# Channel mixer of a streaming-encoder block: gate/up pairs as Strassen products, and GpSimd's weight sums at another place

## The chip, the cores and the metric

The kernel runs on one core of a Trainium2 chip. TensorE (PE) multiplies, with weight loads (PEld) that overlap it; VectorE (DVE), ScalarE (ACT) and GpSimd (POOL) work element by element; DMAs are issued from the queues of SyncE (SP), ACT and POOL. The metric is the device time of one execution in microseconds, the median of several runs.

## The reference

One layer of a residual block on x (512 tokens by 1024 channels, float32). Cut to what matters here:

```python
h = rmsnorm(x, norm1_w)
proj = h @ w_in                                # q, k, v, z, b, a, glu, gates
out_a = gated delta rule, gated norm, @ dn_w_o
c = silu(layernorm(causal_conv31(ga * sigmoid(gb)) + b))
out_b = c @ cm_w_pw2 + cm_b_pw2
x = x + (gate_a * out_a + gate_b * out_b) @ w_out
h2 = rmsnorm(x, norm2_w)
f_gate, f_up = split(h2 @ ffn_w_gate_up)       # 1024 -> 2 x 2816
x = x + (silu(f_gate) * f_up) @ ffn_w_down     # 2816 -> 1024
return rmsnorm(x, norm_f_w)
```

## The kernel before

All products are float32 in three parts. An operand x is split into a high part hi (ACT, a copy rounded to fp32r) and a low part lo = x - hi (DVE, two SBUF inputs), and `split3` (line 107) issues three matmuls: hi by hi, hi by lo, lo by hi. Weights come in units of 128x1024 (`unit`, line 92): a load on SP's queue into `raw`, `whi` on ACT, `wlo` on DVE, each with three buffers. `col_tile` (line 115) multiplies one unit (8 k-steps of 128) with 512 tokens: 24 matmuls of 512 columns.

The program goes through stages. First the input projection with the delta-rule heads and the 31-tap convolution. Then `ln_mean` (line 559) ends the convolution's statistics: GpSimd adds seven squares into `vacc`. The eight columns of `wo` follow, with `ln_norm` (line 575: one reciprocal, then eight products `cv <- cv,pa` on DVE and eight Silu on ACT) in between; the split of its result into `yh` and `yl` reuses the buffers of `wo`'s operand as PE is done with them. Then the eight columns of `wpw`, and `w_out` by tokens (`tok_mm`), whose result is added to x in `y1` and kept in SBUF. `norm2` and `transposes` bring h2 into channel-major form as `hh` and `hl`, in the buffers that the input projection used.

The channel mixer (line 868) runs over f = 0 to 21. Each pair is two columns of 1024, gate `pg` and up `pu`, 48 matmuls of 512 columns; then Silu on ACT and the product `fm` on DVE. For f below 11 = FK, `sums(f)` loads a 1 MB tile `wst` of the down projection's weights on POOL's queue, makes four sums of 128x512 in place on GpSimd and stores them in `wsum`.

The down projection is a product of 2x2 blocks by Strassen's seven products (in Winograd's form) already: halves of the 22 hidden tiles by halves of the tokens, and halves of the hidden tiles by halves of the output. It runs as three passes over FK = 11 units of two products each (`two`, line 931) and a last product, `p3`. Each pass prepares the next operand set (`set2`, `set3`, `set4`) behind its own products. `norm_f` (line 906) makes the closing norm of a token tile and its two output DMAs.

The order of instructions on an engine follows the code and a scheduler's priorities; each engine and each DMA queue takes its instructions in order, and a wait holds up all that is behind it. A tile of a pool with n buffers can't be written until the readers of the tile n before it are done.

Of the kernel before, what the change touches and what calls it, by code (L numbers as in the profile page):

```python
# [6 lines left out]
F32 = mybir.dt.float32  # L7
# [7 lines left out]
P = 128  # L15
T = 512
# [7 lines left out]
PAD3 = 368  # L24
START = 84
# [5 lines left out]
def block_kernel(ctx, tc, a):  # L31
# [6 lines left out]
    pa_ = ctx.enter_context(tc.tile_pool(name="pA", bufs=1))  # L38
# [52 lines left out]

    def unit(ap):
        n = 1024
        raw = wp.tile([P, 1024], F32, name="raw")
        if isinstance(ap, tuple):
            n = T * len(ap)
            for i, p in enumerate(ap):
                nc.sync.dma_start(raw[:, i * T:(i + 1) * T], p)
        else:
            nc.sync.dma_start(raw.rearrange("p (a c) -> p a c", a=2) if len(ap.shape) == 3 else raw, ap)  # L100
        hi = wp.tile([P, 1024], F32R, name="whi")
        marked(S.activation(hi[:, 0:n], raw[:, 0:n], AF.Copy), "unit")  # L102
        lo = wp.tile([P, 1024], F32R, name="wlo")
        marked(V.tensor_tensor(out=lo[:, 0:n], in0=raw[:, 0:n], in1=hi[:, 0:n].bitcast(F32), op=ALU.subtract), "unit")  # L104
        return hi, lo
# [22 lines left out]
    ph1 = ctx.enter_context(ExitStack())  # L128
    psg = ph1.enter_context(tc.tile_pool(name="psg", bufs=2, space=PSUM))
# [7 lines left out]
    with tc.tile_pool(name="st", bufs=2) as st:  # L137
# [74 lines left out]
        def glu0(i):  # L212
# [3 lines left out]
            c = tp.tile([P, T + 30], F32, name="c", bufs=3)  # L216
# [341 lines left out]

    def ln_mean():
# [5 lines left out]
        for i in range(KD):  # L565
# [3 lines left out]
            else:  # L569
                sq2 = tp.tile([P, T], F32, name="acc4")  # L570
                S.activation(sq2, cv[i], AF.Square)
                G.tensor_tensor(out=vacc, in0=vacc, in1=sq2, op=ALU.add)
# [142 lines left out]
    mp.tile([P, PAD], F32, name="pad", bufs=1)  # L715
# [15 lines left out]
    for j in range(KD):  # L731
# [3 lines left out]
        col_tile(ps, a["wo"][j], oh, ol)  # L735
        ma = mp.tile([P, T], F32, name="ma", bufs=KD + 1)
# [19 lines left out]


# [29 lines left out]
    def rms_half(ss, hf, n, cs, sq, last):  # L787
# [44 lines left out]

    tok_mm("wout", KD, mh, ml, norm2, transposes)
    ph2.close()
    keep.close()


    fp = ctx.enter_context(tc.tile_pool(name="fp", bufs=2))
    nfw = fp.tile([P, D], F32, name="nfw", bufs=1)
    nc.gpsimd.dma_start(nfw, a["nfw"].partition_broadcast(P))  # L840
    FK = FF // 2

    def xset():

        return fp.tile([P, T], F32R, name="fh", bufs=FK + 2), fp.tile([P, T], F32R, name="fl", bufs=FK + 2)

# [3 lines left out]

    wsum = [dram.tile([P, 4, T], F32, name="wsum", bufs=FK) for _ in range(FK)]

    def sums(k):
        r = fp.tile([P, 4, T], F32, name="wst", bufs=1)
        nc.gpsimd.dma_start(r, a["wdn"][k].rearrange("p (i c) -> p i c", i=4))
        b11, b12, b21, b22 = (r[:, i, :] for i in range(4))
        G.tensor_tensor(out=b11, in0=b12, in1=b11, op=ALU.subtract)
        G.tensor_tensor(out=b12, in0=b22, in1=b12, op=ALU.subtract)  # L860
        G.tensor_tensor(out=b22, in0=b22, in1=b11, op=ALU.subtract)
        G.tensor_tensor(out=b21, in0=b22, in1=b21, op=ALU.subtract)
        nc.gpsimd.dma_start(wsum[k], r)

    TH = T // 2
    t1, t2 = slice(0, TH), slice(TH, T)
    fms, set1 = [], []
    for f in range(FF):
# [6 lines left out]
        sg = fp.tile([P, T], F32, name="fsg")  # L875
# [5 lines left out]
        fm = fp.tile([P, T], F32, name="fm", bufs=FF)  # L881
        fms.append(fm)
        V.tensor_tensor(out=fm, in0=pu, in1=sg, op=ALU.mult)  # L883
        if f < FK:
            sums(f)
            set1.append(xset())
            hi, lo = (t[:, t1] for t in set1[f])
            xsplit(hi, lo, fm[:, t1])
        else:

            b = fms[f - FK]
            s1 = fp.tile([P, TH], F32, name="s1")
            V.tensor_tensor(out=s1, in0=b[:, t2], in1=fm[:, t2], op=ALU.add)
            hi, lo = (t[:, t2] for t in set1[f - FK])
            xsplit(hi, lo, s1)
            V.tensor_tensor(out=b[:, t2], in0=b[:, t1], in1=b[:, t2], op=ALU.subtract)
            V.tensor_tensor(out=b[:, t1], in0=s1, in1=b[:, t1], op=ALU.subtract)


    hps.close()  # L900
    dp = ctx.enter_context(tc.tile_pool(name="dp", bufs=2, side="right"))
    ss3 = dp.tile([P, 5, NT], F32, name="ss3", bufs=1)
    o0 = [dp.tile([P, T], F32, name="o0", bufs=NT) for _ in range(NT)]
    c1, c2 = slice(0, T), slice(T, D)

    def norm_f(hf, n, cs):
        last = hf == 4 or hf == 1 and n != 1
        rms_half(ss3, hf, n, cs, dp.tile([P, T], F32, name="rms_sq", bufs=1)[:, 0:cs.stop - cs.start], last)
        rs = ss3[:, 3, n:n + 1]
        if hf == 0:  # L910
            G.tensor_tensor(out=o0[n], in0=y1[:, n, cs], in1=nfw[:, cs], op=ALU.mult)
        if last:
            S.activation(o0[n], o0[n], AF.Copy, scale=rs)
            o1 = dp.tile([P, T], F32, name="o1")
            V.scalar_tensor_tensor(out=o1, in0=y1[:, n, c2], scalar=rs, in1=nfw[:, c2], op0=ALU.mult, op1=ALU.mult)
            nc.scalar.dma_start(a["out"][n][:, c1], o0[n])
            nc.sync.dma_start(a["out"][n][:, c2], o1)

    def add(n, cs, what, op=ALU.add, eng=V):
        eng.tensor_tensor(out=y1[:, n, cs], in0=y1[:, n, cs], in1=what, op=op)  # L920
# [149 lines left out]
```

## Time and profile before

| | |
|---|---|
| median of 3 runs | 1000.03 us (997.23 to 1003.04) |
| profiled execution | 1000.16 us, its span 998.4 us |
| mean granted TensorE clock | 0.987 |
| instructions | 13414 |
| HBM read, written | 119.52 MB, 18.10 MB |
| layer norm's statistics, `wo`, `wpw` | about 500 to 590 us |
| `w_out` and norm | about 590 to 643 us |
| channel mixer | about 643 to 870 us |
| down projection | about 870 to 990 us |

How to read it: the span runs from the first to the last instruction; the rest of the execution's time lies around it. Busy time is the time in which an engine worked on instructions of the program. PE's instructions are pipelined: the duration of one (0.39 us for 512 columns) is longer than the step from one start to the next, and the step is what counts in a row of them. A timeline row has the start, the duration, the engine, the line, the operation, the tiles (out<-in) and shapes, and in brackets how long the engine was idle before and who released it. L104 is the split of a weight unit on DVE, L102 the one on ACT, L113 a matmul.

### The profile page before, as it was taken

To read this page: it belongs to the slowest core of one execution; us is meant where nothing else is said; L and a number is where in the kernel's file an instruction comes from. 1 tells how busy PE (TensorE), PEld (TensorE's weight loads), DVE (VectorE), ACT (ScalarE), POOL (GpSimd) and SP (SyncE) were. 2 spreads that over 40 slices of the span, in tenths; PEclk is the share of its full clock that TensorE was granted. 3 is DMA by queue.
4 is the path that set the end of the run, shared out by engine and by line. 5 is a ranking of instruction groups with operands and counts; after the bars stand their busy time and mean duration, and the time that the engine had idled before them with its cause. 6 is when DMAs were issued, how large, how long until landed. Compare 5 with 4: busy or idle time off the path is not lost.

```text
span 998.4 us, 13414 instructions
## 1 busy us (share of the span) xinstructions
PE 963.2 (96%) x4775; PEld 790.2 (79%) x4775; DVE 680.7 (68%) x1044; ACT 508.4 (51%) x1053; POOL 302.1 (30%) x410
## 2 busy tenths in 40 slices
PE   7999889999999999999999999999999999999995
PEld 5687778787887888888878888888888888888784
DVE  4879688899769769998487644643344546468963
ACT  6597366867777665533456322422222322356543
POOL 0423836273453633000040000143534332001412
PEclk9999989999999999999999999999999999999997
DMA  8233323223041222233644432356565664256562
GB/s 320 90 107 97 97 64 97 59 81 117 27 134 58 93 87 64 96 117 134 239 165 148 141 124 85 119 201 241 210 238 195 233 228 143 90 168 191 158 210 84
DMA packets 48290, 138.49 MB, mean 139 GB/s; under 512 B 7472, under 2 KB 9424, under 8 KB 45408
## 3 DMA queue, kind: packets, MB, share of 16 engines
q1 hardware_dynamic: 44016, 112.36, 34.4%
q0 software_dynamic: 3488, 24.17, 6.7%
q10 hardware_dynamic: 720, 1.11, 0.3%
q8 instruction: 37, 0.61, 0.3%
q14 instruction: 29, 0.24, 0.1%
HBM read 119.52 MB, written 18.10 MB: 138 GB/s over the span
## 4 chain that ended last, share of the span: by engine, by line
PE 80%; DVE 9%; POOL 4%; ACT 3%; issue 3%; DMA 1%; SPq 0%; POOLq 0%; ACTq 0%; DVEq 0%
PE mm L113 60%; PE w L113 11%; DVE cv L543 3%; DVE wlo L104 2%; DVE acc L299 1%; POOL Un L349 1%; POOL ytm L375 1%; PE g L345 1%; PE st L482 1%; PE st L494 1%; PE b L414 1%; PE b L420 1%; PE st L480 1%; PE sp L487 1%; ACT Un L348 1%
## 5 line engine op out<-in xcount | busy, mean ns | idle before, releaser
L102 ACT ACTIVATE whi<-raw 128x1024 fp32r<-128x1024 f32 x167 | 176.2, 1057 | 318.5 <-PE mm L113 185.9
L113 PE MATMUL mm<-hh,whi 128*128 128x512 f32 x816 | 328.6, 403 | 0.0
L113 PE MATMUL mm<-hl,whi 128*128 128x512 f32 x816 | 323.4, 396 | 2.3 <-POOL hl L228 1.6
L113 PE MATMUL mm<-hh,wlo 128*128 128x512 f32 x816 | 323.2, 396 | 0.7 <-DVE wlo L104 0.7
L104 DVE TENSOR_TENSOR wlo<-raw,whi 128x1024 fp32r<-128x1024 f32 x167 | 214.4, 1285 | 120.8 <-ACT whi L102 120.2
L543 DVE SCALAR_TENSOR_TENSOR cv<-c,c31w,cv 128x512 f32<-128x512 f32 x240 | 186.5, 803 | 2.1
L113 PEld LDWEIGHTS mm<-hl,whi 128*128 128x128 f32 x816 | 154.5, 189 | 33.0 <-POOL hl L228 2.9
L113 PEld LDWEIGHTS mm<-hh,wlo 128*128 128x128 f32 x816 | 154.2, 189 | 32.7 <-DVE wlo L104 1.1
L113 PEld LDWEIGHTS mm<-hh,whi 128*128 128x128 f32 x816 | 154.5, 189 | 28.7 <-ACT hh L227 0.2
L375 POOL TENSOR_TENSOR ytm<-U,y 128x60 f32<-128x60 f32 (+14 forms) x120 | 57.3, 477 | 44.9 <-DMA U<-sc 36.2
L883 DVE TENSOR_TENSOR fm<-mm,fsg 128x512 f32<-128x512 f32 x21 | 14.5, 692 | 64.9 <-PE mm L113 64.9
L377 POOL TENSOR_TENSOR y<-y,ytm 128x60 f32<-128x60 f32 (+14 forms) x120 | 53.1, 442 | 9.3
L299 DVE SCALAR_TENSOR_TENSOR acc<-mm,c4w,acc 128x511 f32<-128x511 f32 (+2 forms) x72 | 53.2, 739 | 1.3 <-ACT acc L296 0.8
L113 PE MATMUL mm<-yh,whi 128*128 128x512 f32 x128 | 50.6, 396 | 0.0
L113 PE MATMUL mm<-yh,wlo 128*128 128x512 f32 x128 | 49.8, 389 | 0.0
L113 PE MATMUL mm<-yl,whi 128*128 128x512 f32 x128 | 49.8, 389 | 0.0
L113 PE MATMUL w<-whi,fh 128*128 128x512 f32 (+1 forms) x115 | 45.3, 395 | 2.8 <-ACT whi L102 2.8
L113 PE MATMUL w<-wlo,fh 128*128 128x512 f32 (+1 forms) x115 | 45.5, 396 | 2.1 <-DVE wlo L104 2.1
L113 PE MATMUL w<-whi,fl 128*128 128x512 f32 (+1 forms) x115 | 45.0, 393 | 0.0
L791 POOL TENSOR_SCALAR ss<-ss 128x1 f32<-128x1 f32 x17 | 5.7, 336 | 128.6 <-ACT sg L789 116.2
L920 POOL TENSOR_TENSOR A<-A,u 128x512 f32<-128x512 f32 x4 | 6.2, 1578 | 101.9 <-ACT u L951 75.4
L509 POOL TENSOR_TENSOR ss<-ss,half 128x4 f32<-128x4 f32 x8 | 9.5, 1189 | 82.4 <-DVE ss L507 82.4
(288 smaller groups left out, 1506.7 us busy)
## 6 DMA issues: line engine op xcount, KB each, us to landing
raw<-in_win_dram SPq DMA_DIRECT2D x61, 512.0 KB, 3.3
raw<-in_wgu_dram SPq DMA_DIRECT2D x44, 512.0 KB, 3.4
wst<-in_wdn_dram POOLq DMA_DIRECT2D x11, 1024.0 KB, 5.6
wsum<-wst POOLq DMA_DIRECT2D x11, 1024.0 KB, 4.3
raw<-wsum SPq DMA_DIRECT2D x44, 256.0 KB, 3.3
raw<-in_wdn_dram SPq DMA_DIRECT2D x33, 256.0 KB, 3.0
A<-in_x_dram SPq DMA_DIRECT2D x8, 512.0 KB, 6.8
U<-sc SPq DMA_DIRECT2D x64, 64.0 KB, 2.4
```

The source lines that it names most:

```text
L102: marked(S.activation(hi[:, 0:n], raw[:, 0:n], AF.Copy), "unit")
L104: marked(V.tensor_tensor(out=lo[:, 0:n], in0=raw[:, 0:n], in1=hi[:, 0:n].bitcast(F32), op=ALU.subtract), "unit")
L113: marked(PE.matmul(ps, l, r, start=first and i == 0, stop=last and i == 2))
L299: marked(V.scalar_tensor_tensor(out=acc[:, s:], in0=ps[:, :T - s], scalar=c4w[:, j, k:k + 1], in1=acc[:, s:], op0=ALU.mult, op1=ALU.add))
L345: PE.matmul(ps[:, n, :], kT[:, n, :], kT[:, n, :], start=True, stop=True)
L348: S.activation(Un[:, n, :], ps[:, n, :], AF.Copy, scale=nb2[:, n:n + 1])
L349: G.tensor_tensor(out=Un, in0=Un, in1=DT, op=ALU.mult)
L375: G.tensor_tensor(out=tm[:, :, 0:w], in0=U[:, k, :, k + 1:], in1=y[:, :, k:k + 1].broadcast_to([P, NT, w]), op=ALU.mult)
L377: G.tensor_tensor(out=y[:, :, k + 1:], in0=y[:, :, k + 1:], in1=tm[:, :, 0:w], op=ALU.add)
L414: PE.matmul(ps[:, n, 0:16], Ud[:, n, :], xc[:, n, 0:16], start=True, stop=True)
L543: V.scalar_tensor_tensor(out=acc, in0=c[:, k:k + T], scalar=c31w[:, i, k:k + 1], in1=acc, op0=ALU.mult, op1=ALU.add)
L883: V.tensor_tensor(out=fm, in0=pu, in1=sg, op=ALU.mult)
```

## The change

The channel mixer's pairs f = 2 to 21 become Strassen products. The block product is (gate; up) by the two halves of the 1024 channels, times those halves by the two halves of the 512 tokens. Per pair: two loads (`ra`, `rb`); four weight sums of 128x512 on GpSimd into the tiles `s24` and `s31` (two buffers each), so that the raw weights stay whole; four splits (`ra`, the half a22 of `rb`, `s24`, `s31`); seven products `hprod` of 12 matmuls of 256 columns, which go into four PSUM banks; and the sums of the products on DVE, five of which read PSUM. The pairs f = 0 and 1 stay as they were. Behind them the token side is summed once (`xb`, and the operands T1 to T4).

Eight of the down projection's eleven `wsum` tiles are now made behind the layer norm's last add on GpSimd, in four 1 MB buffers `wst` that lie where `hh` and `hl` were; the last three (`held`) are loaded and summed in the first pass of the down projection and stay in SBUF. For the memory, `y1` is stored to DRAM (`ysp`) and read back as `y2`, and the hidden tiles of f = 11 to 21 are stored (`fsp`) and read back in the second pass (`rl`). Two of the operand sums from f = 11 on move from DVE to GpSimd, and one from the third pass to GpSimd in the second. At the end, the closing adds, squares and outputs stand between the products of `p3`.

```diff
+    def sums():
+        for k in range(K2):
+            r = stg.tile([P, 4, T], F32, name="wst")
+            with tc.issue_after(late[0].ins):
+                nc.gpsimd.dma_start(r, a["wdn"][k].rearrange("p (i c) -> p i c", i=4))
+                wsums(r)
+                nc.gpsimd.dma_start(wsum[k], r)
+            yield
...
         col_tile(ps, a["wo"][j], oh, ol)
+        if j in (2, 4, 6, 7):
+            next(summing)
...
         col_tile(ps, a["wpw"][j], yh, yl)
+        if j % 2 == 0:
+            next(summing)
...
+            nc.scalar.dma_start(ysp[n], y1[:, n, :])
...
+    for i, (ks, ts, eng) in enumerate(((kl, t1, V), (kl, t2, V), (kh, t2, V), (kh, t1, G))):
+        xb[i] = fx.tile([P, KH, TH], F32, name="xb%d" % i)
+        sub(xb[i], hh[:, ks, ts].bitcast(F32), hl[:, ks, ts].bitcast(F32), eng, ALU.add)
+    b11, b12, b22, b21 = (xb[i] for i in range(4))
+    sub(b11, b12, b11, V)
+    sub(b12, b22, b12, G)
+    sub(b22, b22, b11, V)
+    sub(b21, b21, b22, V)
...
+    xsplit(*T4, b21)
+    xsplit(*T2, b22)
+    xsplit(*T3, b12)
...
+    def pair(f):
...
+        sub(s31[:, T:], a21, a22, G, ALU.add)
+        sub(s24[:, 0:T], s31[:, T:], a11)
+        sub(s24[:, T:], a12, s24[:, 0:T])
+        sub(s31[:, 0:T], a11, a21)
+        w = wsplit(ra)
+        w22 = wsplit(a22, we)
+        hprod(z[0][:, t1], w, 0, B11)
+        hprod(z[1][:, t1], w, 1, B21)
+        hprod(z[2][:, t1], w22, 0, T4)
+        ws = wsplit(s24)
+        hprod(z[0][:, t2], ws, 0, T2)
+        cw = fq.tile([P, T], F32, name="cw")
+        S.copy(out=cw[:, t1], in_=z[0][:, t1])
+        u = fq.tile([P, TH], F32, name="cu")
+        sub(u, cw[:, t1], z[0][:, t2], V, ALU.add)
+        hprod(z[1][:, t2], ws, 1, B22)
+        w3 = wsplit(s31)
+        hprod(z[3][:, t1], w3, 0, T3)
...
+        sub(v, u, z[3][:, t1], V, ALU.add)
...
+        hprod(z[2][:, t2], w3, 1, T1)
+        sub(cw[:, t2], u, z[2][:, t2], V, ALU.add)
...
+        sub(cw, cw, z[1], V, ALU.add)
+        S.activation(cw, cw, AF.Silu)
+        sub(fm, fm, cw, V, ALU.mult)
...
+        sub(b[:, t2], b[:, t1], b[:, t2])
+        sub(b[:, t1], s1, b[:, t1])
...
     for k in range(K0):
         for n in range(2):
             part(k, n, p3[n], 0, T, k == 0, n == 1 and k == K0 - 1)
+        if k < 2:
+            add(2 + k, c1, p4[k], op=ALU.subtract)
+            squares(0, 2 + k, c1)
+            squares(1, 2 + k, c2, True)
```

DVE's rows for one step of the mixer of before, around the product of f = 11 (engine order; L104 is the split of a weight unit, L883 the product of gate and up, L849 the split of a hidden tile, L893 to L897 the operand sums of the down projection):

```order
L104 TENSOR_TENSOR wlo_7120<-raw_7116,whi_7118 128x1024
L883 TENSOR_TENSOR fm_7074<-mm_7011,fsg_7042 128x512
L893 TENSOR_TENSOR s1_7076<-fm_6227,fm_7074 128x256
L104 TENSOR_TENSOR wlo_7160<-raw_7156,whi_7158 128x1024
L849 TENSOR_TENSOR fl_6237<-s1_7076,fh_6236 128x256
L896 TENSOR_TENSOR fm_6227<-fm_6227 128x256
L897 TENSOR_TENSOR fm_6227<-s1_7076,fm_6227 128x256
L849 TENSOR_TENSOR fl_7835<-fm_6227,fh_7834 128x512
L104 TENSOR_TENSOR wlo_7192<-raw_7188,whi_7190 128x1024
```

Between the products of two pairs stand two weight splits; three operand sums follow each product from f = 11 on. In the changed kernel DVE's rows from the split of `s31` of f = 11 to the last sum of f = 12 (L99 is the split of a weight unit, L903 that of a hidden tile, L906 every sum and product; `cw`, `cu`, `cv2` and `fm2` are the pair's sums, `w` and `mm` are PSUM banks):

```order
L99 TENSOR_TENSOR wlo_7809<-s31_7727,whi_7808 128x1024
L906 TENSOR_TENSOR fm2_7707<-fm2_7707,cw_7660 128x512
L906 TENSOR_TENSOR s1_7712<-fm_6310,fm2_7707 128x256
L99 TENSOR_TENSOR wlo_7867<-raw_7852,whi_7866 128x1024
L903 TENSOR_TENSOR fl_6535<-s1_7712,fh_6534 128x256
L99 TENSOR_TENSOR wlo_7871<-raw_7853,whi_7870 128x512
L906 TENSOR_TENSOR cu_7794<-cw_7792,w_7722 128x256
L99 TENSOR_TENSOR wlo_7911<-s24_7860,whi_7910 128x1024
L906 TENSOR_TENSOR cv2_7824<-cu_7794,w_7725 128x256
L906 TENSOR_TENSOR cw_7792<-cu_7794,w_7724 128x256
L906 TENSOR_TENSOR fm2_7839<-w_7724,cv2_7824 128x512
L906 TENSOR_TENSOR cw_7792<-cw_7792,w_7723 128x512
```

A pair now has four splits, three of 1024 columns and one of 512 (`raw_7853`, the half a22), and five sums that read PSUM (`w`, `mm`). Between the split of `s31` and the sum `cu` stand the product, one operand sum `s1`, the split of `ra` (`raw_7852`), that of the hidden tile and that of a22, all with two SBUF inputs. Two of the three operand sums are gone from this queue.

GpSimd's rows in the mixer of before, for one f below 11 (the load and the store of a `wst` tile around its four sums in place):

```order
L857 DMA wst_6229<-in_wdn_dram 128x2048
L859 TENSOR_TENSOR wst_6229<-wst_6229 128x512
L860 TENSOR_TENSOR wst_6229<-wst_6229 128x512
L861 TENSOR_TENSOR wst_6229<-wst_6229 128x512
L862 TENSOR_TENSOR wst_6229<-wst_6229 128x512
L863 DMA wsum_6166<-wst_6229 128x2048
```

and GpSimd's in the changed kernel, for one pair from f = 11 on (the four weight sums into `s31` and `s24`, and the two operand sums `fm`):

```order
L906 TENSOR_TENSOR s31_7995<-raw_7987 128x512
L906 TENSOR_TENSOR s31_7995<-raw_7986,raw_7987 128x512
L906 TENSOR_TENSOR s24_7994<-s31_7995,raw_7986 128x512
L906 TENSOR_TENSOR fm_6310<-fm_6310 128x256
L906 TENSOR_TENSOR s24_7994<-raw_7986,s24_7994 128x512
L906 TENSOR_TENSOR fm_6310<-s1_7712,fm_6310 128x256
```

The six DMAs and sums that came once for each f below 11 are gone from the mixer; four sums of the weights that come next stand in every pair, and from f = 11 on the two sums that left DVE's queue, one on either side of the last weight sum.

Where the `wst` sums went on GpSimd: the changed kernel's rows behind the layer norm's adds (L580), with the loads (L741), the four sums of a tile (L732 to L735), and the first store (L743):

```order
L580 TENSOR_TENSOR sacc_5015<-sacc_5015,acc4_5043 128x512
L741 DMA wst_5203<-in_wdn_dram 128x2048
L741 DMA wst_5301<-in_wdn_dram 128x2048
L732 TENSOR_TENSOR wst_5203<-wst_5203 128x512
L741 DMA wst_5378<-in_wdn_dram 128x2048
L733 TENSOR_TENSOR wst_5203<-wst_5203 128x512
L732 TENSOR_TENSOR wst_5301<-wst_5301 128x512
L734 TENSOR_TENSOR wst_5203<-wst_5203 128x512
L733 TENSOR_TENSOR wst_5301<-wst_5301 128x512
L735 TENSOR_TENSOR wst_5203<-wst_5203 128x512
L734 TENSOR_TENSOR wst_5301<-wst_5301 128x512
L743 DMA wsum_5058<-wst_5203 128x2048
```

The add shown is the last of seven; of two buffers in turn, the sums of one stand between those of the other. In the kernel before nothing follows the seventh add on GpSimd until `norm2`.

More of the change, by code (lines that the diff above doesn't have):

```diff
@@ L24 @@
 PAD3 = 368
+PAD4 = 506
 START = 84
@@ L557, in gate @@
         yield
+    late = []
     def ln_mean():
@@ L880, in block_kernel @@
             k_loop(*first[1], slice(2 * P, T))
[L881 to L897, printed above, removed]
+        V.tensor_tensor(out=hidden(f), in0=pu, in1=sg, op=ALU.mult)
@@ L1010, in block_kernel @@
         add(1, cs, ps)
-        norm_f(4 if c else 1, 1, cs)
+        squares(4 if c else 1, 1, cs, c)
+        if not c:
+            out(0)
+    out(1)
 def _layout(i):
```

263 lines of the change are left out of this document (185 added, 78 removed).

## The prediction

> **What bounds the kernel now.** I read the page first, then the windows, then the timelines of the stages that the change touches.
>
> ```profile
> span 998.4 us, 13414 instructions
> PE 963.2 (96%) x4775; PEld 790.2 (79%) x4775; DVE 680.7 (68%) x1044; ACT 508.4 (51%) x1053; POOL 302.1 (30%) x410
> PE 80%; DVE 9%; POOL 4%; ACT 3%; issue 3%; DMA 1%; SPq 0%; POOLq 0%; ACTq 0%; DVEq 0%
> ...
> 740.00:780.00 40.00, 40.00 (x178) 33.14 (x177) 19.24 (x20) 12.07 (x17) 16.17 (x15) 1.00 0.62 222
> ...
> 979.30:986.00 6.70, 5.65 (x17) 4.25 (x16) 4.06 (x5) 2.65 (x5) 0.55 (x1) 0.50 0.20 78
> ```
>
> PE is 96% busy and makes 80% of the chain that ended last. In the channel mixer (the window from 740 on; columns are PE, PEld, DVE, ACT, POOL, clock, DMA) PE is busy all 40 us at full clock, DVE under half, POOL 40%. So there only PE time counts, and a change pays if it shortens PE and keeps the others under PE. The last row is the tail, where the clock is at half.
>
> **Strassen's gain on PE.** Two timelines give the pace, start to start, first DVE at the end of a pair, then PE in the one stretch that has 128x256 products.
>
> ```profile
> 691.74 0.69 DVE L883 TENSOR_TENSOR fm<-mm,fsg 128x512 f32<-128x512 f32 x1 [2.94 <-PE mm L113]
> 702.62 0.69 DVE L883 TENSOR_TENSOR fm<-mm,fsg 128x512 f32<-128x512 f32 x1 [3.37 <-PE mm L113]
> 703.46 1.87 DVE L104 TENSOR_TENSOR wlo<-raw,whi 128x1024 fp32r<-128x1024 f32 x1 [0.15 <-ACT whi L102]
> 705.25 1.50 DVE L849 TENSOR_TENSOR fl<-fm,fh 128x256 fp32r<-128x256 f32 x1
> ...
> 713.50 0.69 DVE L883 TENSOR_TENSOR fm<-mm,fsg 128x512 f32<-128x512 f32 x1 [3.37 <-PE mm L113]
> 714.34 1.23 DVE L104 TENSOR_TENSOR wlo<-raw,whi 128x1024 fp32r<-128x1024 f32 x1 [0.15 <-ACT whi L102]
> 715.48 0.42 DVE L849 TENSOR_TENSOR fl<-fm,fh 128x256 fp32r<-128x256 f32 x1
> ...
> 635.13 0.28 PE L113 MATMUL w<-hh,whi 128*128 128x256 f32 x1
> ...
> 640.39 0.28 PE L113 MATMUL w<-hh,wlo 128*128 128x256 f32 x1
> ```
>
> A pair (48 products of 512 columns) takes 702.62 - 691.74 = 10.88 us. From 635.13 to 640.39 there are 44 steps: 0.1195 us for a product of 256 columns, weights changed as often as in the new code. A new pair is 7 x 12 = 84 such products: 84 x 0.1195 = 10.04 us. Twenty pairs (f = 2 to 21) would save 20 x 0.84 = **16.8 us**, if PE stays the bound.
>
> **DVE and GpSimd per pair.** This decides. While GpSimd's weight sums ran, DVE was held up:
>
> ```profile
> 702.95 1.30 POOL L860 TENSOR_TENSOR wst<-wst 128x512 f32<-128x512 f32 x1
> 704.33 2.14 POOL L861 TENSOR_TENSOR wst<-wst 128x512 f32<-128x512 f32 x1
> 706.55 1.36 POOL L862 TENSOR_TENSOR wst<-wst 128x512 f32<-128x512 f32 x1
> ```
>
> The DVE subtraction of 256 columns takes 0.42 us with GpSimd idle (715.48) and 1.50 beside L861 (705.25): it waits 1.09. L861 itself waits behind the 1024-column subtraction (2.14 against 1.30). The two engines take turns. The product L883, which reads PSUM and one SBUF tile, takes 0.69 both beside L859/L860 (702.62) and alone (713.50): it doesn't wait. So each GpSimd sum costs DVE 1.09 us if a DVE operation with two SBUF inputs is ready, and nothing beside a PSUM one.
>
> DVE per new pair, start to start (a 1024 row is followed after 715.48 - 714.34 = 1.14 us; I take 0.60 for 512 and 0.34 for 256, their 0.69 and 0.42 less the same 0.09): three 1024 splits 3.42; the a22 split, two PSUM adds and the last product at 512, 2.40; three PSUM adds and one split at 256, 1.36. That is **7.18 us**, from f = 11 on 7.52 (s1 more). GpSimd has four sums of 512 (1.30 each) and from f = 11 on two of 256 (I take half). ACT has three whi of 1057 ns (the page's group below), one of half that, and some 1.7 us of small work: 5.4, under PE.
>
> ```profile
> L102 ACT ACTIVATE whi<-raw 128x1024 fp32r<-128x1024 f32 x167 | 176.2, 1057 | 318.5 <-PE mm L113 185.9
> ```
>
> When do they meet? GpSimd's sums for the pair after next wait until DVE's split of s31 frees that tile. At that moment DVE's next rows (in the order shown for the change) are the product, s1, the 1024 split, the 256 split and the a22 split: all two SBUF inputs, all ready. So three sums cost 1.09 each, the fourth falls partly beside the PSUM add u (1.09 - 0.34 = 0.75); from f = 11 on a half-size one costs 0.55, the last falls beside PSUM adds. DVE's period is 7.18 + 3.27 + 0.75 = 11.20, later 7.52 + 3.27 + 0.55 + 0.75 = 12.09: above PE's 10.04, so DVE becomes the bound. 9 x 11.20 + 11 x 12.09 = 233.8 against 20 x 10.88 = 217.6: **+16 us**.
> Ends: if every sum finds DVE in PSUM work or idle, the shared turns alone are 4.96 + 4 x 1.09 = 9.32 (then PE's 10.04) and 5.30 + 5 x 1.09 = 10.75: 208.6, or -9. If nothing overlaps, 7.18 + 4 x 1.30 = 12.38 and 7.52 + 5 x 1.30 = 14.02: 265.6, or +48. I take the middle because the order fixes who is ready; it is nearest to rows 703 to 707, where every operation met another.
>
> The Trainium skill, "SBUF — State Buffer", section "SBUF: two separate sides", says that DVE operations with two SBUF inputs and GpSimd share a port pair as an exclusive lock held for the whole instruction. By that rule a wait may reach all of L860's 1.30; the trace has 1.09, and the estimate by the rule would be some 0.9 us more a pair.
>
> **The sums behind the layer norm.** Eight of eleven move there; GpSimd runs them from about 522 us (its seven adds end at 516.08, then a load).
>
> ```profile
> 503.20 12.88 POOL L572 TENSOR_TENSOR sacc<-sacc,acc 128x512 f32<-128x512 f32 x7 [19.22 <-ACT acc L571]
> ...
> wst<-in_wdn_dram POOLq DMA_DIRECT2D x11, 1024.0 KB, 5.6
> ...
> 519.24 3.36 DVE L580 RECIPROCAL pa<-pa 128x512 f32<-128x512 f32 x1 [0.78 <-ACT pa L579]
> 522.75 0.69 DVE L737 TENSOR_TENSOR ma<-mm,gsl 128x512 f32<-128x512 f32 x1 [0.16 <-PE mm L113]
> 523.36 4.90 DVE L582 TENSOR_TENSOR cv<-cv,pa 128x512 f32<-128x512 f32 x8
> 528.19 0.69 DVE L737 TENSOR_TENSOR ma<-mm,gsl 128x512 f32<-128x512 f32 x1
> 528.80 1.22 DVE L104 TENSOR_TENSOR wlo<-raw,whi 128x1024 fp32r<-128x1024 f32 x1
> ...
> 533.63 0.69 DVE L737 TENSOR_TENSOR ma<-mm,gsl 128x512 f32<-128x512 f32 x1 [0.76 <-PE mm L113]
> ...
> 541.08 3.70 DVE L726 TENSOR_TENSOR yl<-cv,yh 128x512 fp32r<-128x512 f32 x6
> ...
> 625.19 1.09 ACT L823 ACTIVATE hh<-mm 128x512 fp32r<-128x512 f32 x2 [0.29 <-PE mm L821]
> ```
>
> PE doesn't stop here before. The eight products from 523.36 come with eight waits: 8.7 us less GpSimd's two DMA issues, about 8, and the split behind them (ready 530.0) waits once more: ready at 539. It belongs to the column that PE begins at 533.6 (the product at 533.63 marks the end of the column before), three buffers on. PE stops about 5 us. The eight yl splits from 541.08, paced by PE, wait likewise, up to 8.7 with some slack: 4. Sum **+9**, between 0 (the loads come late) and 13. 32 sums at 1.3 to 2.1 last until 565 to 590, before the next user of their memory at 625.
>
> **The start of the pairs.** DVE and GpSimd must make three operand sums before the first pair, where before nothing was needed.
>
> ```profile
> 641.78 1.29 DVE L824 TENSOR_TENSOR hl<-mm,hh 128x512 fp32r<-128x512 f32 x2 [0.60 <-ACT hh L823]
> ...
> 659.10 0.69 DVE L883 TENSOR_TENSOR fm<-mm,fsg 128x512 f32<-128x512 f32 x1 [3.42 <-PE mm L113]
> ```
>
> hl is whole at 643; PE is done with f = 1 at 659.1. GpSimd's queue until it has b12: one add of 1024, six weight sums, one subtraction of 1024, or 2 x 2.6 + 6 x 1.3 = 13 alone, about 17 with turns: 660. Then th1, tl1, tl0, tl2 and the pair's own split (1.06 + 4 x 1.14) are all in front of PE's first product: 666 to 668. **+8**, between 1 and 13.
>
> **The down projection.** Three 1 MB tiles and 2 MB of spilled rows are loaded in one run on SP's queue ahead of the eighth unit; at the page's best slice (320 GB/s) that is 16 us. That unit is due 7 x 12 x 0.227 = 19 us into the pass (0.227 is 10.88 / 48); the run starts about 6 us in, since the load ahead of it takes the buffer of the fourth unit, whose split waits for the first unit's products (2.7), then ACT and DVE. **+3**, 0 to 8. The spills on ACT's queue cost nothing: ACT has 5 us free a pair.
>
> ```profile
> GB/s 320 90 107 97 97 64 97 59 81 117 27 134 58 93 87 64 96 117 134 239 165 148 141 124 85 119 201 241 210 238 195 233 228 143 90 168 191 158 210 84
> ```
>
> **The tail.** PE waited here, and then ran at half clock for 6.7 us (quoted above), a loss of about 3.3:
>
> ```profile
> 979.00 0.60 PE L113 MATMUL w<-whi,fh 128*128 128x512 f32 x1 [2.83 <-ACT whi L102]
> ...
> 981.08 0.80 PE L113 MATMUL w<-wlo,fh 128*128 128x512 f32 x1 [1.05 <-DVE wlo L104]
> ```
>
> Together 7.2. The change moves the closing adds, squares and outputs between the last products, so most goes; the splits still stand behind outputs that wait for GpSimd. **-5**, 0 to -7.
> The stops of some 5 and 8 us above can halve the clock as this one did: **+2**, 0 to 7.
>
> **Sum.** 1000.16 (the profiled execution: span 998.4 and 1.76 around it; the median of the runs is 1000.03) + 16 + 9 + 8 + 3 - 5 + 2 = **1033**.
>
> **Rivals.**
> 1. *PE stays the bound.* DVE's period stays under 10.04 if a weight sum costs it less than (10.04 - 7.18)/4 = 0.72, later (10.04 - 7.52)/5 = 0.50: GpSimd's sums fall beside PSUM adds instead of behind s31's split. Then -16.8, with 4 at the layer norm, 4 at the start, -5 in the tail and 0 elsewhere: 986. For it: DVE has 2.5 to 2.9 us free. Against: the moment at which s31 comes free.
> 2. *About even.* Each sum costs 0.9 early and 0.7 late, so pairs take 10.8 to 11.0; the other terms halve: 1000.
> 3. *Nothing overlaps*: 12.38 and 14.02 a pair: +48 instead of +16: 1065.
> 4. *The clock.* PE now stops for one to two us in each pair; in the tail a stop of 2.83 brought 6.7 us at half. If the clock halves for 6.7 us in each pair, PE loses 3.3 there, 1.3 more than DVE leaves idle: 20 x 1.3 = 26 more, 1059. The Trainium skill, "TensorE: Matmul & The Clock Gate", section "A second HAM failure mode: psum-queue depth-cycling", says that frequent short idles between groups of products can make the clock swing; no stretch of this trace shows it in a regular loop.
> That the products don't shorten PE's own time is no rival: the 0.1195 is in the trace.
>
> **How the numbers follow.** Forecast 0.60 (likeliest 1010 to 1055), rival 1 0.13, rival 2 0.12, rival 3 0.10, rival 4 0.05. A measurement of this kernel can tell about 0.5% (5 us) from no change. Faster: rival 1 and little of 2: 0.15. Same: most of 2 and the low end of the forecast: 0.12. Slower: 0.73. The range leaves out half of rival 1 below, and half of 3 and of 4 above: 988 to 1062.
>
> **What would show it.** In the pairs: PE under 90% busy, pairs 11 to 12 us apart and longer from f = 11 on; DVE's 1024 splits at about 2.3 us, PSUM adds unchanged, PE waiting on wlo. If pairs are 10.0 to 10.1 apart and PE is full, my account of who is ready is wrong. Around 534 to 560: PE stops behind wlo and yl; around 660: a stop of several us behind tl or wlo. In the tail: no stop of 2.8 us.

## The result, and the profile after

The changed kernel takes 1037.88 us (median of 4 runs, 1029.58 to 1043.93), the kernel before 999.25 (4 runs): a ratio of 1.0376, 95% interval 1.0295 to 1.0458. It is slower by 39 us, 5 us above the forecast of 1033. The profiled execution took 1035.75, its span is 1034.0. The page's lines that answer to those of before, and two rows of the table of windows (columns: window, length, then busy time of PE, PEld, DVE, ACT, POOL with the number of instructions, granted clock, DMA share, GB/s):

```profile
span 1034.0 us, 15332 instructions
PE 962.1 (93%) x5495; PEld 817.3 (79%) x5495; DVE 855.4 (83%) x1172; ACT 547.8 (53%) x1124; POOL 482.2 (47%) x517
740.00:780.00 40.00, 37.86 (x299) 36.16 (x299) 40.00 (x39) 16.26 (x23) 25.97 (x15) 1.00 0.32 104
810.00:890.00 80.00, 70.98 (x558) 67.97 (x559) 79.37 (x82) 29.71 (x45) 63.43 (x40) 1.00 0.32 106
```

In the same window from 740 on, DVE went from 19.24 of 40 us to all 40. (A row counts as busy while it is held up by GpSimd, so not all of these 40 us are work; the rows below tell the two apart.) PE looks nearly as busy as before, but its count tells: 299 products in 40 us, where the pace of 0.1195 would give 335. PE is no longer the bound in the mixer; DVE is.

The timeline of the changed kernel (start, duration, engine, line, operation, tiles; idle time before and releaser in brackets), one pair with f below 11 on DVE and GpSimd, then the Silu of two pairs with f above 11 and of the last three pairs on ACT. In this kernel L118 is a matmul, L1085 and L1086 are the splits of the down projection's weights on ACT and DVE, L790 is an add behind `wpw`:

```profile
755.43 1.98 DVE L99 TENSOR_TENSOR wlo<-s,whi 128x1024 fp32r<-128x1024 f32 x1
...
759.19 1.21 DVE L99 TENSOR_TENSOR wlo<-s,whi 128x1024 fp32r<-128x1024 f32 x1
760.33 0.68 DVE L906 TENSOR_TENSOR fm<-fm,cw 128x512 f32<-128x512 f32 x1
760.48 3.93 POOL L906 TENSOR_TENSOR s<-raw 128x512 f32<-128x512 f32 x2 [4.16 <-DVE wlo L99]
760.98 2.27 DVE L99 TENSOR_TENSOR wlo<-raw,whi 128x1024 fp32r<-128x1024 f32 x1
763.17 1.52 DVE L903 TENSOR_TENSOR fl<-fm,fh 128x256 fp32r<-128x256 f32 x1
...
764.61 1.78 DVE L99 TENSOR_TENSOR wlo<-raw,whi 128x512 fp32r<-128x512 f32 x1
766.31 0.41 DVE L906 TENSOR_TENSOR cu<-cw,w 128x256 f32<-128x256 f32 x1
766.64 1.97 DVE L99 TENSOR_TENSOR wlo<-s,whi 128x1024 fp32r<-128x1024 f32 x1
...
817.14 0.63 ACT L1018 ACTIVATE cw<-cw 128x512 f32<-128x512 f32 x1 [5.87 <-DVE cw L906]
829.22 0.63 ACT L1018 ACTIVATE cw<-cw 128x512 f32<-128x512 f32 x1 [5.87 <-DVE cw L906]
...
889.66 0.63 ACT L1018 ACTIVATE cw<-cw 128x512 f32<-128x512 f32 x1 [5.87 <-DVE cw L906]
...
898.42 0.63 ACT L1018 ACTIVATE cw<-cw 128x512 f32<-128x512 f32 x1 [3.44 <-DVE cw L906]
...
906.24 0.63 ACT L1018 ACTIVATE cw<-cw 128x512 f32<-128x512 f32 x1 [1.49 <-DVE cw L906]
```

GpSimd's first sum starts when the split of `s31` (759.19) is done. From there on four DVE operations are longer than alone: 2.27 against 1.21, 1.52 against 0.42, 1.78 against 0.68, 1.97 against 1.21, together 4.02 us, and the sum `cu` from PSUM between them is 0.41 as ever. From split to split it is 766.64 - 755.43 = 11.21 us, and from Silu to Silu at f above 11 it is 12.08. The forecast had 11.20 and 12.09. The last two steps are shorter, 8.76 and 7.82.

Where the 35.6 us between the two spans lie, by PE's first product of each stage:

| stage | before | after | difference | forecast |
|---|---|---|---|---|
| up to `wo` | 499.4 | 500.2 | +0.7 | 0 |
| `wo` and `wpw` | 88.4 | 93.3 | +4.9 | +9, with the next row |
| `w_out` | 46.2 | 50.6 | +4.4 (1.7 of it half clock) | |
| norm, f = 0 and 1 | 24.8 | 25.9 | +1.1 | 0 |
| from the end of f = 1 to the pairs' running, with the half clock | 0 | 10.6 | +10.6 | +8 |
| pairs f = 2 to 21 | 217.6 | 223.0 | +5.4 | +16 |
| down projection | 113.8 | 123.3 | +9.6 (5.0 of it half clock) | +3 - 5 |
| behind the last product | 8.2 | 7.1 | -1.1 | |

The clock's term, +2 in the forecast, is inside the rows. The total was nearly right, its parts were not, and that their errors cancel is luck. The pairs cost some 11 us less than forecast, the down projection and the clock together some 13 more (8.5 with what lies behind the last product, and 4.2 of half clock elsewhere, for a forecast of 3 - 5 + 2 = 0). Luck of a second kind is in the 4.4 us of `w_out`: the traces of e1 and e4, which leave that stage as it is, have 46.15 us there, as before the change, and from `wo` to the end of `w_out` 139.04 and 139.10 us instead of 143.85. PE's rows at the stops, with the DVE row that waited ahead of the pairs, the queue of loads in the down projection, and the closing rows of GpSimd's sums behind the layer norm (the same timeline):

```profile
524.13 10.54 DVE L590 TENSOR_TENSOR cv<-cv,pa 128x512 f32<-128x512 f32 x8
...
530.69 1.74 POOL L734 TENSOR_TENSOR wst<-wst 128x512 f32<-128x512 f32 x1
...
556.00 8.11 DVE L790 TENSOR_TENSOR acc<-acc,ma 128x512 f32<-128x512 f32 x1
556.04 1.30 POOL L733 TENSOR_TENSOR wst<-wst 128x512 f32<-128x512 f32 x1
...
562.28 1.28 POOL L734 TENSOR_TENSOR wst<-wst 128x512 f32<-128x512 f32 x1
...
589.27 4.87 DVE L790 TENSOR_TENSOR acc<-acc,ma 128x512 f32<-128x512 f32 x1
...
596.56 0.50 PE L118 MATMUL w<-wlo,ma 128*128 128x512 f32 x1 [2.51 <-DVE wlo L99]
...
669.01 2.29 DVE L906 TENSOR_TENSOR xb<-xb,xb 128x1024 f32<-128x1024 f32 x1 [6.04 <-POOL xb L906]
678.12 0.58 PE L118 MATMUL w<-hh,wlo 128*128 128x256 f32 x1 [6.55 <-DVE wlo L99]
...
911.53 1.28 SPq L1094 DMA_DIRECT2D held<-in_wdn_dram  x3
912.86 3.13 SPq L1094 DMA_DIRECT2D y<-ysp  x4
916.09 0.50 SPq L1082 DMA_DIRECT2D raw<-in_wdn_dram  x1
931.35 1.58 ACT L1085 ACTIVATE whi<-raw 128x1024 fp32r<-128x1024 f32 x2 [7.89 <-DMA raw<-wsum]
932.46 0.80 PE L118 MATMUL w<-whi,fh 128*128 128x512 f32 x1 [9.66 <-ACT whi L1085]
```

The eight products `cv` take 10.54 us for 4.90, 5.6 more, where the forecast had about 8. The row at 556.00 wasn't foreseen: an add of 0.69 us is held for 8.11 while six sums run beside it without a pause (1.27 to 1.30 each). A second one, of 4.87 at 589.27, delays the split that PE waits for at the start of `w_out`. At 669.01 DVE has waited 6.04 us for GpSimd's `b12`. The run of loads starts at 911.53, 8.0 us into the pass, and the weights queued behind it at 916.09 are split at 931.35.

### The profile page after: what moved, and what is told of

The parts are those of the page before. It is cut to its first block, busy times and chain, and to the rows that moved or that the text cites. A ratio compares the mean times of both kernels' runs of the same rounds, so it can differ in the third digit from the quotient of the medians.

```text
span 1034.0 us, 15332 instructions
## 1 busy us (share of the span) xinstructions
PE 962.1 (93%) x5495; PEld 817.3 (79%) x5495; DVE 855.4 (83%) x1172; ACT 547.8 (53%) x1124; POOL 482.2 (47%) x517
## 5 line engine op out<-in xcount | busy, mean ns | idle before, releaser
L118 PE MATMUL mm<-hh,whi 128*128 128x512 f32 (+1 forms) x616 | 237.6, 386 | 0.0
L118 PE MATMUL mm<-hl,whi 128*128 128x512 f32 (+1 forms) x616 | 232.4, 377 | 2.3 <-POOL hl L234 1.6
L118 PE MATMUL mm<-hh,wlo 128*128 128x512 f32 (+1 forms) x616 | 232.2, 377 | 2.3 <-DVE wlo L99 2.3
L99 DVE TENSOR_TENSOR wlo<-raw,whi 128x1024 fp32r<-128x1024 f32 (+1 forms) x134 | 198.1, 1481 | 41.2 <-ACT whi L98 40.7
L98 ACT ACTIVATE whi<-raw 128x1024 fp32r<-128x1024 f32 (+1 forms) x134 | 131.9, 986 | 115.2 <-PE mm L118 86.5
L118 PEld LDWEIGHTS mm<-hh,wlo 128*128 128x128 f32 x616 | 116.8, 190 | 21.6 <-DVE wlo L99 2.7
L118 PEld LDWEIGHTS mm<-hl,whi 128*128 128x128 f32 x616 | 117.4, 191 | 20.3 <-POOL hl L234 2.9
L118 PEld LDWEIGHTS mm<-hh,whi 128*128 128x128 f32 x616 | 117.4, 191 | 16.4 <-ACT hh L233 0.2
L906 POOL TENSOR_TENSOR s<-raw 128x512 f32<-128x512 f32 x40 | 70.9, 1791 | 67.9 <-DVE wlo L99 67.9
L118 PE MATMUL w<-hh,wlo 128*128 128x256 f32 x232 | 67.8, 292 | 16.0 <-DVE wlo L99 16.0
L118 PE MATMUL w<-hh,whi 128*128 128x256 f32 x232 | 66.6, 288 | 1.3 <-ACT whi L98 1.0
L118 PE MATMUL w<-hl,whi 128*128 128x256 f32 x232 | 66.5, 287 | 1.0 <-DVE hl L866 1.0
L99 DVE TENSOR_TENSOR wlo<-s,whi 128x1024 fp32r<-128x1024 f32 x40 | 61.9, 1547 | 0.4 <-ACT whi L98 0.4
L118 PEld LDWEIGHTS w<-hh,wlo 128*128 128x128 f32 x232 | 45.5, 196 | 18.2 <-DVE wlo L99 18.1
L118 PE MATMUL w<-whi,fh 128*128 128x512 f32 (+1 forms) x115 | 46.3, 403 | 9.7 <-ACT whi L1085 9.7
L1086 DVE TENSOR_TENSOR wlo<-raw,whi 128x1024 fp32r<-128x1024 f32 (+1 forms) x30 | 38.8, 1297 | 16.9 <-ACT whi L1085 16.7
L118 PE MATMUL mm<-yh,wlo 128*128 128x512 f32 x128 | 50.1, 391 | 2.2 <-DVE wlo L99 2.1
```

What stands on the lines that cost most here:

```text
L98: marked(S.activation(hi, raw, AF.Copy), "unit")
L99: marked(V.tensor_tensor(out=lo, in0=raw, in1=hi.bitcast(F32), op=ALU.subtract), "unit")
L118: marked(PE.matmul(ps, l, r, start=first and i == 0, stop=last and i == 2))
L906: eng.tensor_tensor(out=out, in0=in0, in1=in1, op=op)
L1086: V.tensor_tensor(out=lo[:, c], in0=r, in1=hi[:, c].bitcast(F32), op=ALU.subtract)
```

## The experiments

Each is the changed kernel with one edit, or with several where that is said. "Alone" means a row without GpSimd work beside it. Ratios are against the kernel before, run beside each experiment, with their 95% intervals. Because single executions differ by a stop more or less (the 4.4 us in `w_out` are absent in e1 and e4, which don't touch that stage), I compare stage by stage in the traces and use the totals only for the last versions.

**e1: the pairs' weight sums on DVE.**

```diff
-        sub(s31[:, T:], a21, a22, G, ALU.add)
-        sub(s24[:, 0:T], s31[:, T:], a11)
+        sub(s31[:, T:], a21, a22, V, ALU.add)
+        sub(s24[:, 0:T], s31[:, T:], a11, V)
...
```

> The four weight sums of every pair go from GpSimd to DVE, nothing else. Theory (turns): the pairs are long because a GpSimd sum and a DVE operation with two SBUF inputs take turns, 1.09 us of DVE a sum, where DVE itself needs 0.60. Then the 1024-column splits come back from 1.55-2.27 to about 1.21 us, the pairs f = 3 to 11 are 10.05 to 10.2 us apart (DVE's own 7.18 + 4 x 0.60 = 9.58, under PE's 10.04), f = 12 to 19 10.5 to 11.0 (two operand sums are still on GpSimd), and the time falls by 20 to 28 us, to about 1012. Rival 1 (DVE's rows are their own length, it simply has too much work): a pair grows by 2.4, to 13.6, the time by about 45. Rival 2 (the chain through the two buffers of s31 sets the pace, not DVE's occupation): pairs stay within 0.3 of 11.2 and 12.1, with DVE idle in them.

Measured: 1001.93 us, ratio 1.0019 (0.9994 to 1.0043): the whole loss is gone, though DVE has more to do. Its timeline: DVE in one pair, and ACT's first copy in pairs further on:

```profile
756.43 1.22 DVE L99 TENSOR_TENSOR wlo<-s,whi 128x1024 fp32r<-128x1024 f32 x1
...
761.99 1.23 DVE L99 TENSOR_TENSOR wlo<-raw,whi 128x1024 fp32r<-128x1024 f32 x1
763.13 0.42 DVE L903 TENSOR_TENSOR fl<-fm,fh 128x256 fp32r<-128x256 f32 x1
763.47 0.68 DVE L99 TENSOR_TENSOR wlo<-raw,whi 128x512 fp32r<-128x512 f32 x1
...
723.58 0.37 ACT L1002 COPY cw<-w 128x256 f32<-128x256 f32 x1 [0.83 <-PE w L118]
733.66 0.37 ACT L1002 COPY cw<-w 128x256 f32<-128x256 f32 x1 [0.93 <-PE w L118]
...
836.57 0.35 ACT L1002 COPY cw<-w 128x256 f32<-128x256 f32 x1
847.21 0.35 ACT L1002 COPY cw<-w 128x256 f32<-128x256 f32 x1
```

Every split has its own length again. Below f = 12 a pair takes 733.66 - 723.58 = 10.08 us, PE's pace (84 x 0.12); above, where DVE is still the bound, 10.64. Rival 1 (13.6) and rival 2 (11.2 and 12.1, unchanged, with DVE idle) are out. The gain was larger than expected, 36 us for 20 to 28, partly because the stop ahead of the pairs fell from 6.55 to 1.14 us (GpSimd's queue no longer holds weight sums there, so `b12` comes earlier), partly because this execution has no stop in `w_out`. From the end of f = 1 to the down projection its trace takes 203.0 us instead of 233.7.

**e8: one of the four sums back on GpSimd.** As e1, but:

```diff
-        sub(s31[:, T:], a21, a22, V, ALU.add)
+        sub(s31[:, T:], a21, a22, G, ALU.add)
```

> As e1, but the first of the four weight sums of a pair (a21 + a22) is on GpSimd again. It takes 0.60 us off DVE and adds one turn. Theory (a turn costs DVE 1.09 us beside an operation with two SBUF inputs, nothing beside one that reads PSUM): where DVE is the bound, f = 12 to 19, a pair of 10.64 goes to 11.1 if the sum meets the splits as it did, or to 10.1 if it falls beside PSUM sums; in the rows one splits' or sums' duration is about 1.0 longer, and the time moves by less than 6 us either way. Rival (a GpSimd sum costs DVE less than DVE's own 0.60): the pairs shorten to 10.1 with no DVE row of two SBUF inputs longer than alone.

Measured: 1013.32 us, ratio 1.0128 (1.0099 to 1.0156), 11 us over e1, where less than 6 was expected. The timeline, f above 11:

```profile
816.17 0.41 DVE L906 TENSOR_TENSOR s<-fm,fm 128x256 f32<-128x256 f32 x1
...
816.66 1.65 POOL L906 TENSOR_TENSOR fm<-fm 128x256 f32<-128x256 f32 x1 [0.97 <-DVE s L906]
817.64 0.95 DVE L903 TENSOR_TENSOR fl<-s,fh 128x256 fp32r<-128x256 f32 x1
818.52 1.23 DVE L99 TENSOR_TENSOR wlo<-raw,whi 128x512 fp32r<-128x512 f32 x1
...
825.61 1.67 POOL L906 TENSOR_TENSOR s<-raw 128x512 f32<-128x512 f32 x1 [6.41 <-DVE wlo L99]
826.05 1.78 DVE L906 TENSOR_TENSOR s<-raw 128x512 f32<-128x512 f32 x1
827.75 0.41 DVE L906 TENSOR_TENSOR s<-fm,fm 128x256 f32<-128x256 f32 x1
```

The sum holds DVE for 1.78 - 0.68 = 1.10 us, the 1.09 of the forecast. The operand sums meet DVE as well (0.95 for 0.41, 1.23 for 0.68: 1.09 together). A pair takes 827.75 - 816.17 = 11.58 us, more than the 11.1 expected, which had only the one sum cost more than in e1; where PE is the bound, below f = 12, it stays at 10.08. Eight pairs of 11.58 instead of 10.64 make 7.5 us of the loss; from the end of f = 1 to the down projection it is 13.2 in the traces (216.2 against 203.0), with a stop of 3.37 us ahead of the pairs for 1.14. Where it meets a DVE row with two SBUF inputs, a sum on GpSimd costs DVE more than doing it: 1.10 against 0.60.

**e2: the operands' start on DVE.**

```diff
-    ... (kh, t2, V), (kh, t1, G))):
+    ... (kh, t2, V), (kh, t1, V))):
...
-    sub(b12, b22, b12, G)
+    sub(b12, b22, b12, V)
```

> The two token-side operations on GpSimd ahead of the first Strassen pair (the add xb3 and the subtraction b12) go to DVE. Theory (GpSimd's queue): b12 stands behind six weight sums there, and DVE waits 6.04 us for it. Then that wait is gone, PE's stop of 6.55 us at the first pair falls to 3 or less, the half clock behind it shortens or goes, the pairs stay 11.20 and 12.09 apart, and the time falls by 4 to 9 us. Rival (DVE's own backlog with turns sets the start): the stop stays above 5 us and the time within 2 us.

Measured: 1028.86 us, ratio 1.029 (1.0258 to 1.0323). The median is 9.0 us lower, at the end of the range expected, but the traces show less of it in this stage. DVE's wait of 6.04 is gone, and PE's stop is split rather than removed:

```profile
672.71 0.35 PE L118 MATMUL w<-th,whi 128*128 128x256 f32 x1 [2.55 <-issue]
674.45 0.58 PE L118 MATMUL w<-tl,whi 128*128 128x256 f32 x1 [1.38 <-DVE tl L903]
```

With 6.83 us at half clock (10.24 in the changed kernel), the way from the end of f = 1 to the down projection shortened by only 2.5 us (233.7 to 231.2). The theory named the right wait, but since DVE sets the pace there, what counts is its work: it gave up 6.04 us of waiting and took on two operations and more turns: from 650 to the first pair's splits seven of its rows of 1.21 us take 2.3 beside eight GpSimd sums, where five of the changed kernel's do (2.2 to 2.3). e1 shows the better half: with the sums off GpSimd, `b12` can stay there.

**e3: no sums behind the layer norm.** The 32 sums of the eight tiles are left out, their loads and stores stay.

```diff
-                wsums(r)
                 nc.gpsimd.dma_start(wsum[k], r)
```

> The 32 sums of the eight tiles behind the layer norm are left out; their loads and stores stay. Theory (turns with DVE): from the first product of wo to the end of w_out the changed kernel takes 143.85 us (500.15 to 644.00), the kernel before 134.6; without the sums it is 134.5 to 136, the eight products cv take 4.9 us instead of 10.54, and the stop of 2.51 at the start of w_out with its half clock goes; the time falls by 8 to 10 us. Rival (the 16 MB of loads and stores hold up the weight loads): that stretch stays above 141 us.

Measured: 1028.47 us, ratio 1.0285 (1.0253 to 1.0317). From `wo` to the end of `w_out` it takes 134.98 us (501.29 to 636.27; 143.85 with the sums, 134.6 before). The eight products `cv` take 4.90 us. Waits of PE in that stretch (us in total, number, longest), changed kernel and e3:

```profile
PE w L118 <- DVE wlo L99: 2.8, 2, 2.5
PE mm L118 <- DVE wlo L99: 2.1, 1, 2.1
PE mm L118 <- DVE yl L761: 1.2, 2, 0.8
```

```profile
PE w L118 <- DVE wlo L99: 0.3, 1, 0.3
```

16 MB of loads and stores still flow, so the rival is out: the sums on GpSimd cost the 9 us of this trace of the changed kernel. Half of them, the stop at `w_out`, come and go with the same sums: in e1 and e4 they cost 4.5 (139.04 and 139.10).

**e4: the `y2` loads in the second pass**, with the adds that need them.

```diff
-        + [(y2[:, n, :], ysp[n]) for n in range(NT)])
...
-    two(lambda k: (wt(k, 3), wt(k, 1)), set2, p6 + p7, set_3)
+    two(lambda k: (wt(k, 3), wt(k, 1)), set2, p6 + p7, set_3y, [(y2[:, n, :], ysp[n]) for n in range(NT)])
```

> The four loads of the spilled rows (2 MB) go from the first pass of the down projection to the second, with the adds that need them. Theory (one run of 5 MB on SP's queue ahead of the eighth unit): a run of 3 MB lasts some 12 us instead of 19.8, PE's stop of 9.66 us falls to 1 to 4, the half clock behind it shortens or goes, and the time falls by 6 to 12 us. Rival (the passes need more bytes than the memory gives): the stop goes to the second pass or comes back there in the same size, and the time stays within 3 us.

Measured: 1026.82 us, ratio 1.0288 (1.0242 to 1.0334), but the down projection itself shortened by only 3.6 us (123.3 to 119.7). The stop halved, and another came:

```profile
920.28 0.79 PE L118 MATMUL w<-whi,fh 128*128 128x512 f32 x1 [4.46 <-ACT whi L1085]
933.28 0.50 PE L118 MATMUL w<-wlo,fh 128*128 128x512 f32 x1 [2.33 <-DVE wlo L1086]
```

Between theory and rival: neither is settled by it.

**e5: three edits together**, e1's, e4's, and the sums behind the layer norm on DVE, behind the last product `cv` (`late[1]`), one tile for each column of `wpw`:

```diff
+                with tc.issue_after(late[1].ins):
+                    wsums(r, V)
```

> Three edits together: the pairs' weight sums on DVE (as in e1), the y loads in the second pass (as in e4), and the 32 sums behind the layer norm on DVE, behind the last product cv, one tile for each column of wpw. Theory (turns and the run of loads are separate costs, so the gains add): 1002 of e1, less 7 to 9 for the layer norm's stretch (143.85 us now, 134.98 with the sums left out; on DVE 135 to 138), less 6 to 10 for the loads: 985, between 980 and 990, faster than before by 1 to 2%; pairs as in e1, 10.08 and 10.64 to 10.7 apart. Rival (DVE, which takes its queue in order, is held up by a sum that waits for its load): the stretch stays above 140 us with PE stops behind wlo or yl, and the time is 990 to 1000.

Measured: 992.53 us, ratio 0.9918 (0.9900 to 0.9936): faster than the kernel before by 0.8%, at 2.5 us above the range. The stretch from `wo` to `w_out` is 134.6 us (500.39 to 635.00), without a stop: 32 sums cost nothing on DVE. The gains did add: against e1's trace the stretch falls from 139.04 to 134.60 and the down projection from 124.2 to 119.8, 4.4 us each. Both were put too high: the loads at 6 to 10, and the layer norm's 7 to 9 was taken from the changed kernel's trace, which has the stop at `w_out` that e1's doesn't have.

**e6: two held tiles on ACT's queue**, and the second pass's closing adds on DVE. As e5, and the sums of the held tiles also stand behind other units of the first pass (2, 4 and 6 instead of 2, 3 and 4).

```diff
+        if k in (0, 2):
+            i = k // 2 + 1
+            nc.scalar.dma_start(held[i].rearrange("p i c -> p (i c)"), a["wdn"][K2 + i])
```

> As e5, and two of the three held tiles are loaded from ACT's queue behind the first and the third split of the first pass, and the closing adds of the second pass that stand on GpSimd (u and v) go to DVE. Theory (a run of loads in one queue, and DVE waiting for v's buffer until GpSimd has added): the stops of 4.46 and 2.33 us that e4 has in the first pass fall to 3 in all or less, the stop of 2.5 at the start of the third pass to 1 or less; 4 to 7 us less than e5. Rival (the first pass is limited by GpSimd's sums of the held tiles or by the bytes, not by the queue): the stops of the first pass stay at 5 to 7 us in all, and only the third pass gains, some 3 us.

Measured: 990.22 us, ratio 0.9903 (0.9880 to 0.9925), 2.3 us under e5 for 4 to 7 expected; in the traces the down projection gains 0.4 (119.8 to 119.4). The stops of the first pass are 4.66, 1.50 and 1.95, 8.1 in all: the theory of the queue falls. ACT's rows, and one of DVE's behind them:

```profile
870.39 0.36 ACTq L1115 DMA_DIRECT2D held<-in_wdn_dram  x1
...
872.42 0.34 ACTq L1115 DMA_DIRECT2D held<-in_wdn_dram  x1
...
885.13 1.06 ACT L1083 ACTIVATE whi<-raw 128x1024 fp32r<-128x1024 f32 x1 [8.32 <-DMA raw<-wsum]
...
888.34 1.77 DVE L901 TENSOR_TENSOR fl<-fm,fh 128x512 fp32r<-128x512 f32 x1
```

The two left ACT's queue 2 us apart, since its rows run ahead of PE there, and ACT still waited 8.32 us for the next weights. Another queue didn't help here, where the bytes come at the same time. The stop of 4.66 stands behind that load; those of 1.50 and 1.95 stand behind DVE's splits, which are held up beside GpSimd's sums of the held tiles (1.77 us for 0.68). At the start of the third pass the stop fell from 2.02 to 0.80.

**e7: no held tiles.** As e5, with the adds of e6; all eleven tiles are summed on DVE ahead of the mixer, the last three in the first half of `w_out`.

```diff
-    FK, K2 = FF // 2, 8
+    FK, K2 = FF // 2, FF // 2
...
+    def late_sum():
+        k, r = rest3.pop(0)
+        with behind(mybir.EngineType.PE):
+            wsums(r, V)
+        nc.gpsimd.dma_start(wsum[k], r)
...
+                if hf == 0 and rest3:
+                    late_sum()
```

> As e5 with v's and u's adds on DVE as in e6, and no held tiles: all eleven weight-sum tiles are made on DVE ahead of the mixer, the last three inside the first half of w_out. Theory (the bytes that arrive in the first pass, 3 MB of held tiles among them, are what makes the eighth unit late): the stops of the first pass (4.66, 1.5 and 1.95 us in e6) fall to 1 or less in all, with no half clock there; the stretch of wo, wpw and w_out stays at 134.5 to 138; the time is 8 to 12 us under e6, 978 to 982. Rival (three more tiles are too much for the stages before: DVE waits for their loads ahead of w_out's splits): a stop of 3 us or more about the first units of w_out, and the time is 985 or more.

Measured: 983.28 us, ratio 0.9827 (0.9801 to 0.9852), the fastest of all, 1.7% under the kernel before, 1.3 us above the range expected and 6.9 under e6 (8 to 12 expected). In the first pass PE has no stop and no half clock; the down projection takes 110.0 us (113.8 before the change). The stretch from `wo` to `w_out` is 137.1 us (497.03 to 634.17), 2.5 more than in e6, with a stop at the head of `w_out`, smaller than the rival's 3:

```profile
599.22 0.50 PE L118 MATMUL w<-wlo,ma 128*128 128x512 f32 x1 [1.97 <-DVE wlo L99]
```

With 3 MB fewer in the first pass its stop is gone, as the theory of the bytes has it; 12 GpSimd sums went with them. By e6's rows the stop of 4.66 was the bytes' and the other two in the main the sums'; no run takes away one without the other.

## Why the prediction was right, and where it was not

- **Strassen on PE: right.** 10.08 us a pair in e1 for a forecast of 10.04.
- **DVE becomes the bound: right, in mechanism and size.** 4.02 us of waiting a pair for 3.27 + 0.75, periods of 11.21 and 12.08; e1 takes the waits away with the sums, e8 brings one back at 1.10. That the order fixes who is ready when `s31` comes free stands in the rows, and was not varied in a run. Of the signs named, "PE under 90% busy" came only from f = 11 on (71.0 of 80 us); below it PE's rows fill 37.9 of 40 us, though it is not the bound.
- **The sum over the pairs, +16: too high by some 11 (+5.4).** The step "9 x 11.20 + 11 x 12.09" counted sums for every pair. The last two have none to make for a pair after next: the Silu rows are 8.76 and 7.82 us apart at the end (2.46 us of GpSimd work each), 7.6 less. f = 11 still had the shorter period, 0.9 less. The other 2 or so I put down to PE's lead at either end; no run shows it apart.
- **Layer norm, +9: met by luck (9.3), not in its places.** Of the 5 us in front of `wo`'s column 2.1 came, of the 4 behind `yl` 1.2; the stop at `w_out` (2.51, with 1.7 of half clock) was not foreseen, and without it the sums cost 4.5 us (e1 and e4): the term was twice too high for what it named. The sums lasted until 598, not 565 to 590.
- **Start of the pairs, +8: right.** 8.2 us from the end of f = 1 until PE runs (stops of 1.01 and 6.55), behind `b12`; the half clock adds 2.5. PE started at 678, later than the 666 to 668 I had, since DVE waited for GpSimd until 669 and f = 1 ended 11 us later than before.
- **Down projection, +3: mis-sized, a stop of 9.66.** The run began 8.0 us in, not 6, and lasted 19 to 20 us, not 16. I had left out a 0.5 MB load from GpSimd's queue that falls into it (issued at 911.80, landed at 921.28); at the 320 GB/s of the forecast it is 1.6 us, an estimate. The stop of 3.04 at the start of the third pass was not foreseen; e6 has 0.80 there and e7, with the same adds on DVE, 2.9, so its cause stays open.
- **Tail, -5: right in kind.** No stop in it. Without the two stops and the half clock of its passes (9.66, 3.04 and 5.0) the down projection would take 105.6 us, some 8 less than the 113.8 before.
- **The clock, +2: mis-sized, about 9** (the 1.7 at `w_out` is in the 9.3 above as well)**.** 1.7 at `w_out`, 2.5 at the start, 3.3 in the first and 1.7 in the third pass. I had one episode in mind; there were four, one at each stop of 2.5 us or more.
- **Two sums among the rivals are off.** Rival 2's pairs cost 0.6 us and its halved terms 8.5, which makes 1009 and not 1000. Rival 4's 1.3 us a pair hold from f = 11 on; below it, where DVE's period is 1.2 above PE's, it is 2.1, and the twenty pairs make 33 us and not 26. The forecast rests on neither.

## What to carry to other kernels

An engine that has time isn't free help: price a moved operation by what it costs the engine that it takes turns with, here 1.1 us of DVE for a sum that DVE itself makes in 0.6. When an algorithm takes work off the bound engine, first add up the next engine row by row with those waits in it, and check the ends of the loop, where the extra work stops. Loads that aren't needed in a stage should not be issued in it; another queue didn't change that here.

## What the runs showed of the hardware

- GpSimd and DVE mostly alternate: in the pairs, and also from 529 to 535, where the sums of two tiles stand in turn and none needs the one before it (1.72 to 1.76 us each beside `cv` products of 1.77 to 1.79). But the sums of two tiles in turn also kept DVE out for a whole run: 8.11 us for six, 4.87 for an add that takes 0.69 alone, and again 8.10 in e2 and 4.87 in e4. What decides between the two is open. The Trainium skill, "SBUF — State Buffer", section "SBUF: two separate sides", has the lock held for one instruction; that agrees with the 1.09 to 1.10 of a 1.30 sum, and doesn't give waits over six.
- The reverse holds too: in e8 one GpSimd sum took 4.35 us beside DVE operations without a pause.
- PE's stops of 0.54 us in each pair, later 1.15, left the clock at 1.00 (the windows above), so rival 4 did not come. The swing that the Trainium skill, "TensorE: Matmul & The Clock Gate", section "A second HAM failure mode: psum-queue depth-cycling", tells of did not show here.
- Of single stops behind 480 us, those of 3.3 us or more all brought half clock, those of 1.8 to 3.2 some (1.79 in e8 and 3.04 here did, 2.12 here and 2.9 in e7 didn't). The half clock lasted 3.41 us or a multiple of it wherever it ended inside the span. The Trainium skill, "TensorE: Matmul & The Clock Gate", section "What's actually happening", has a free-running window of 3413 ns; the lengths in the traces agree. By that page, the same stop could fall either way; no run here varies it.
